# Fox attention: one of four modulation vectors summed on GpSimd instead of VectorE

## The chip, the core and the metric

The kernel runs on one core of a Trainium2 chip. A core has TensorE (matmuls; PE in the profile, with PEld for its weight loads), VectorE (DVE), ScalarE (ACT), GpSimd (POOL) and SyncE (SP), whose queue issues all of this kernel's DMAs in order. The metric is the device time of one execution in microseconds, lower is better.

## What is computed

A trunk of two layers over 1024 tokens of 1024 channels: layer 0 mixes tokens by forgetting attention (16 heads of 64), layer 1 by gated linear attention, each followed by a SwiGLU network. Every sub-layer is modulated by six vectors of 1024 numbers, computed from one conditioning vector `c`:

```python
c_act = jax.nn.silu(c)
for i in range(DEPTH):
    mod = c_act @ ada_w[i] + ada_b[i]              # ada_w[i]: 1024 x 6144
    sh1, sc1, g1, sh2, sc2, g2 = jnp.split(mod, 6, axis=-1)
    h = modulate(rms_norm(x, norm1_g[i]), sh1, sc1)
    ...
    x = x + g1[:, None, :] * y
    h = modulate(rms_norm(x, norm2_g[i]), sh2, sc2)
    x = x + g2[:, None, :] * swiglu(h, ffn_w_in[i], ffn_w_out[i])
```

In the attention, per head and block of 128 queries, the logits are the scaled scores plus differences of a cumulative sum, masked causally; then softmax, then the product with the values.

## The kernel before

Matmuls run in three passes over a high and a low part of each operand (`mm3`, L285; the parts are made by `split` and by the weight loads, L205). Layer 0's attention runs in eight pairs of heads, `attention(p)` (L1207). A pair has two heads `a` and for each four units `g` in the order 0, 3, 1, 2 (L1195); a unit is two query blocks, 2g and 2g+1. `scores(u)` (L1112) of a unit does, for each of its two blocks: score matmuls (L1132, L1133) and a mask matmul (L1135) on TensorE; the sum with the cumulative row and a running minimum on VectorE (L1138); the exponential on ScalarE (L1142); the reciprocal of its sum on VectorE (L1143); and the division, which multiplies the row of probabilities by that reciprocal on GpSimd (L1144), in place, 128 x 128 up to 128 x 1024 numbers. The unit before it is then finished (`finish`, L1199; `outputs`, L1147): transposes of the probabilities (L1164), their split on ScalarE and VectorE (L174, L175), products with the values (L1176, L1178), and the sum into the output tile (L1193). The probabilities live in a ring of three slots, `lpr`.

Beside pair p's attention, `weave` (L130) lays the projections for pair p+1: queries and keys (`qk_proj`, L1097), evacuated by `q_evac` and `k_evac` (L760, L770: two clearings on GpSimd, copies on ScalarE, differences on VectorE), and values (`v_half`). Beside pair 7 it lays the first part of the output projection (`fox_tail`, L1307). Attention with these runs from about 102 to 612 us of the span; then come the rest of the output projection and the two SwiGLU networks with the second mixer between them.

Weights are loaded as 512 KB tiles into a ring of three slots, `wr`, and split: the high part on ScalarE (L223), the low part in four quarters, three on GpSimd and one on VectorE (L227). Up to three weights are fetched ahead.

Two of layer 0's modulation vectors are made at the start. The other four, 2 to 5, are summed during the attention by `ada_steps` (L411). Each vector is the sum of 32 rows of 128 x 256 numbers; row o is a tile of `ada_w` times a column of the activated `c` (`c42`). One `ada_steps` loads four rows at a time by four DMAs of 128 KB (L423) into a slot of the same ring `wr`, and adds them on VectorE, one instruction a row (L442 the first, L444 the others). It ends with two small matmuls (L449) and an addition (L452). Vector 2 gates the attention's output (L1277, pair 7 and after), 3 and 4 modulate the second norm, 5 gates the SwiGLU network's output.

A `Pace` (L458) says where in the program these steps are called for: `ada0(3.3)` behind each of the projections of queries and keys from `qk_proj(2, 0)` on (L1108), twelve calls, each worth 3.3 steps; four vectors have 36 steps. The order of the instructions on each engine is made when the program is built: a scheduler takes from all that its model of the engines holds ready, the earlier in the program first, so an instruction can run well ahead of the place where it is called for, if its data and its slot are there. Data, ring slots and a few written orders (`in_order`, the lags of `weave` on TensorE) bound this. On the chip each engine's order is fixed.

Of the kernel before, what the change touches and what calls it, by code (L numbers as in the profile page):

```python
# [9 lines left out]
F32 = mybir.dt.float32  # L10
# [4 lines left out]
ALU = mybir.AluOpType  # L15

P = 128
S = 1024
D = 1024
ND = D // P  # L20
HALF = 512
# [32 lines left out]
def trunk(ctx, tc, x, c, ada_w, ada_b, norm1_g, norm2_g, ffn_w_in, ffn_w_out,  # L54
          fox_w_in, fox_b_f, fox_w_out, gla_w_in, gla_w_a2, gla_b_a, gla_g_o,
          gla_w_out, final_g, out, dbg=None, stop=None):
    nc = tc.nc
# [51 lines left out]
    def psl(t, n=1):  # L109
        return slice(t * P, (t + n) * P)  # L110
# [55 lines left out]
    four = cst.tile([P, 4], F32, name="four")  # L166
# [104 lines left out]
    class Weights:  # L271
# [36 lines left out]
    acc_r = Ring(big, acc_sl)  # L308
# [65 lines left out]
    for t in range(6):  # L374
        nt, src = (4, rows2[0:8, :]) if t < 4 else (2, crow)
# [4 lines left out]
    vec = cst.tile([P, 160], F32, name="vec")  # L380
    cact = cst.tile([P, 8], F32, name="cact")
    c42 = cst.tile([P, 64], F32, name="c42")
# [10 lines left out]
    modc = cst.tile([P, 2, 6, 8], F32, name="modc")  # L393
# [8 lines left out]
    def make_a(l, i, ks=slice(0, 8)):  # L402
        j = 1 if i == 0 else 4
        g0 = 96 + i * 16 + l * 8
        nc.vector.scalar_tensor_tensor(amul[:, l, i, ks], modc[:, l, j, ks], 1.0,
                                       vec[:, g0:g0 + 8][:, ks], op0=ALU.add, op1=ALU.mult)

    def last_of(e):
        return next(i for i in reversed(nc.cur_bb.bb.instructions) if i.engine == ENG[e])

    def ada_steps(l, j, acc, raw_of, nt, ahead):  # L411


        steps, got = deque(range(32 // nt)), deque()

        def load():
            if not steps:
                return
            n = steps.popleft()
            raw = raw_of([P, nt * 256], F32, f"ada{l}{j}{n}").rearrange("p (t c) -> p t c", t=nt)  # L420
            src = ada_w[l, 32 * nt * n:32 * nt * (n + 1), j * D:(j + 1) * D]
            for q in range(4):
                nc.sync.dma_start(raw[32 * q:32 * q + 32],  # L423
                                  src[:, 256 * q:256 * q + 256].rearrange("(r t) c -> r t c", t=nt))
            got.append(raw)

        for _ in range(ahead):
            load()
        for n in range(32 // nt):
            load()  # L430
            if ahead:
                yield ADA_A
            raw = got.popleft()
            with ExitStack() as es:
                if ahead:
                    es.enter_context(tc.issue_after(last_of("D")))
                elif n == 0:
                    es.enter_context(tc.issue_after(split_after["D"]))
                for t in range(nt):
                    o = (0 if nt == 4 else 32) + t * (32 // nt) + n  # L440
                    if n == t == 0:
                        nc.vector.tensor_scalar(acc, raw[:, t], c42[:, o:o + 1], None, op0=ALU.mult)  # L442
                    else:
                        nc.vector.scalar_tensor_tensor(acc, raw[:, t], c42[:, o:o + 1], acc,  # L444
                                                       op0=ALU.mult, op1=ALU.add)
            yield ADA_B if ahead else 1.0
        mp = pj([P, 2, 4], F32, f"mp{l}{j}")
        for b in range(2):
            nc.tensor.matmul(mp[:, b], acc[:, psl(b)], four, start=True, stop=True)  # L449
        o = l * 48 + j * 8  # L450
        qb = lambda t: t.rearrange("p (q b) -> p b q", b=2)
        nc.vector.tensor_add(qb(modc[:, l, j]), mp, qb(vec[:, o:o + 8]))  # L452
        for i, jj in ((0, 1), (1, 4)):
            if j == jj:
                make_a(l, i)
        yield 1.0

    class Pace:  # L458
# [18 lines left out]
            while self.q:  # L477
                self(1.0)

    ada0, ada1 = Pace(), Pace()  # L480

    def ada1_queue(js, acc, raws_):
        r = Cycle(raws_)
# [254 lines left out]
    sr, tr, orr, pj = ps_rings(2, 3, 1, 2)  # L738
# [8 lines left out]
    def qk_tiles(p):  # L747


        at = {nm: qk_free.popleft() for nm in ("QA", "QB", "KA")}  # L750
        if p:
            before = qk_at.pop(p - 1)
            at.update(zip(("KB", "KLA", "KLB"), (before[nm] for nm in ("QA", "KA", "KLA"))))
            qk_free.extend(before[nm] for nm in ("QB", "KB", "KLB"))
        else:
            at.update({nm: qk_free.popleft() for nm in ("KB", "KLA", "KLB")})
        qk_at[p] = at
        return {nm: big.tile([P, S], FR, tag=sl, name=f"{nm}{p}") for nm, sl in at.items()}
# [202 lines left out]
    def load_cum(h):  # L961
        cums[h] = cumr([P, S], F32, f"cum{h}")
        nc.sync.dma_start(cums[h], cum_d[h].partition_broadcast(P))
# [82 lines left out]
    for n, (d, hf) in enumerate(rest0):  # L1046
# [23 lines left out]
        if n in late_tr:  # L1070
            tp, i = late_tr[n]
# [25 lines left out]
    def qk_proj(p, i):  # L1097

        if i == 0:
            qkt[p] = qk_tiles(p)  # L1100
        wt = feed.next()
        feed.depth = 3
        for hf in range(2):
            ps = pj([P, HALF], F32, f"qk{i}{p}{hf}")
            yield from proj(ps, wt, hT, hf)
            (k_evac if i else q_evac)(ps, qkt[p], hf)
        if p > 1:
            ada0(3.3)  # L1108

    oTs = {}  # L1110

    def scores(u):  # L1112

        p, a, g = u
        t = qkt[p]
        Qs, K1, KL = (t["QA"], t["KA"], t["KLA"]) if a == 0 else (t["QB"], t["KB"], t["KLB"])
        cm = cums[2 * p + a]
        if g < 2:
            both = lpr([P, (4 * g + 3) * P], F32, f"lp{p}{a}{g}")
            lps = [both[:, 0:(2 * g + 1) * P], both[:, (2 * g + 1) * P:]]  # L1120
        else:
            lps = [lpr([P, (2 * g + 1 + i) * P], F32, f"lp{p}{a}{g}{i}") for i in range(2)]
        st = sm.tile([P, 2, 4], F32, tag="st", bufs=4, name=f"st{p}{a}{g}")
        for qi in range(2):
            qb = 2 * g + qi
            qs, lp, Wd, mcur = psl(qb), lps[qi], (qb + 1) * P, 3e38
            cuts = (0, 384, 640) if Wd == 640 else (0, Wd) if Wd <= HALF else (0, HALF, Wd)
            for n_, (k0, k1) in enumerate(zip(cuts, cuts[1:])):
                ps = sr([P, k1 - k0], F32, f"s{p}{a}{qb}{k0}")
                early = u == (0, 0, 0)  # L1130
                diag = k1 == Wd
                nc.tensor.matmul(ps, Qs[:, qs], K1[:, k0:k1], start=True, stop=False)  # L1132
                nc.tensor.matmul(ps, Qs[:, qs], KL[:, k0:k1], start=False, stop=not diag)  # L1133
                if diag:
                    nc.tensor.matmul(ps[:, k1 - k0 - P:], identb, maskb, start=False, stop=True)  # L1135
                mnew = st[:, qi, n_:n_ + 1]
                with tc.issue_after(v_last) if early else ExitStack():
                    nc.vector.tensor_tensor_reduce(lp[:, k0:k1], ps, cm[:, k0:k1], 1.0, mcur,  # L1138
                                                   ALU.add, ALU.min, mnew)
                mcur = mnew  # L1140
                yield max(0.22, 0.00085 * (k1 - k0))
            nc.scalar.activation(lp, lp, AF.Exp, bias=mcur, scale=-1.0, accum_out=st[:, qi, 2:3])  # L1142
            nc.vector.reciprocal(st[:, qi, 3:4], st[:, qi, 2:3])  # L1143
            nc.gpsimd.tensor_scalar(lp, lp, st[:, qi, 3:4], 1.0, op0=ALU.mult, op1=ALU.mult)  # L1144
        return lps
# [61 lines left out]
    def attention(p):  # L1207
        for a in range(2):
            for g in ORDER:
                u = (p, a, g)  # L1210
                lps = yield from scores(u)
                if pending[0] is not None:
                    yield from finish(*pending[0])
                pending[0] = (u, lps)
        if p == 7:
            yield from finish(*pending[0])
# [2 lines left out]
        for g in gs:  # L1219
            yield from g  # L1220

    acc0 = acc_r([P, 2, HALF], F32, "acc0")[:, 0, 0:256]
    for j in (2, 3, 4, 5):
        ada0.q.append(ada_steps(0, j, acc0, wr, 4, 0))
    run(v_half(0, 0, gates_end))
    q_evac(accs[1][1][1], qkt[0], 1)
# [4 lines left out]
    for p in range(7):  # L1231
# [4 lines left out]
        load_cum(2 * p + 2)  # L1236
        load_cum(2 * p + 3)
    ada0.flush()


    def dump(name, tiles):
# [555 lines left out]
    pj, atr, kvr, opr, trr = ps_rings(3, 1, 1, 2, 1)  # L1797
# [336 lines left out]
```

## Time and profile before

| what | us |
|---|---|
| median of 3 executions (lowest, highest) | 2398.98 (2395.54, 2399.1) |
| the profiled execution, its own time | 2397.77 |
| its span, first to last instruction | 2396.1 |
| VectorE busy in the span | 1776.6 |
| GpSimd busy in the span | 1008.5 |

The profile is one execution. A row of a group gives line, engine, operation, out<-in with shapes and the count, then the busy time and the mean ns of one, then the idle time of the engine just before and what ended it. A row of the waits says who waited for whom: the sum in us, the times, the longest. A row of the timeline gives start, duration, engine and instruction; `[1.43 <-DMA ...]` is idle time before it and what ended that. PE's ends are modelled, so what its rows show for certain is when it started, and when it stood idle. The granted clock of TensorE is 0.997 of full speed over this execution.

### The profile page before, as it was taken

How to read it: one execution, taken by the hardware profiler on the slowest of the kernel's cores; microseconds unless marked ns; L12 is line 12 of the kernel's file. 1: busy time of each engine (PE TensorE's matmuls, PEld its weight loads, DVE VectorE, ACT ScalarE, POOL GpSimd, SP SyncE). 2: the span in 40 equal slices, each digit the busy share in tenths (PEclk: the TensorE clock that was granted, in tenths of full speed). 3: DMA queues.
4: the chain of work that ended last, by engine and by line, in shares of the span. 5: the costliest groups of instructions: out<-in, count | busy, mean ns of one | idle time of the engine just before them, and what ended most of it. 6: DMA issues, size and time to landing. Idle time of an engine off the chain costs nothing.

```text
span 2396.1 us, 35784 instructions
## 1 busy us (share of the span) xinstructions
PE 2368.3 (99%) x12344; PEld 2016.8 (84%) x12344; DVE 1776.6 (74%) x3016; ACT 1127.8 (47%) x2164; POOL 1008.5 (42%) x911
## 2 busy tenths in 40 slices
PE   8999999999999999999999999999999999999998
PEld 7888888888888888888888888898888888888888
DVE  6577878886698788876798666655687877775787
ACT  6666555674443333345325645353343333345326
POOL 1333333333445666643264321222345666643262
PEclk9999999999999999999999999999999999999999
DMA  7422424342435544557655242334424544457664
GB/s 254 145 89 90 131 84 128 106 138 83 150 109 173 179 166 165 171 196 261 229 187 162 67 119 80 107 112 135 136 96 161 183 145 159 154 182 256 228 202 146
DMA packets 335773, 363.42 MB, mean 152 GB/s; under 512 B 24348, under 2 KB 277432, under 8 KB 335592
## 3 DMA queue, kind: packets, MB, share of 16 engines
q1 hardware_dynamic: 335592, 361.15, 45.9%
q8 instruction: 97, 1.59, 0.3%
q14 instruction: 84, 0.69, 0.1%
HBM read 268.19 MB, written 92.86 MB: 151 GB/s over the span
## 4 chain that ended last, share of the span: by engine, by line
PE 90%; DVE 5%; DMA 2%; ACT 1%; issue 1%; POOL 0%; SPq 0%; DVEq 0%; POOLq 0%; ACTq 0%
PE p_b L288 16%; PE p_b L286 16%; PE p_b L287 16%; PE t_b L1164 2%; PE o_b L1178 2%; PE qk_b L286 2%; PE qk_b L287 2%; PE qk_b L288 2%; PE vps_b L286 1%; PE vps_b L288 1%; PE vps_b L287 1%; PE s_b L1132 1%; PE s_b L1133 1%; PE gr_b L286 1%; PE gr_b L287 1%
## 5 line engine op out<-in xcount | busy, mean ns | idle before, releaser
L175 DVE TENSOR_TENSOR o_s<-xv_s,o_s 128x512 fp32r<-128x512 f32 (+1 forms) x376 | 324.1, 867 | 66.1 <-ACT o_s L174 65.6
L174 ACT CAST o_s<-xv_s 128x512 fp32r<-128x512 f32 (+1 forms) x376 | 216.2, 587 | 303.6 <-PE p_b L288 248.0
L287 PE MATMUL p_b<-B,o_s 128*128 128x512 f32 x608 | 237.8, 391 | 0.0
L288 PE MATMUL p_b<-B,o_s 128*128 128x512 f32 x608 | 237.5, 391 | 0.0
L286 PE MATMUL p_b<-B,o_s 128*128 128x512 f32 x608 | 236.3, 392 | 0.0
L1144 POOL TENSOR_SCALAR lp_s<-lp_s,st 128x128 f32<-128x128 f32 (+7 forms) x128 | 99.0, 778 | 291.1 <-DVE st L1143 280.7
L843 POOL TENSOR_TENSOR ex_s<-xv_s,xv_s 128x512 f32<-128x512 f32 (+1 forms) x64 | 85.5, 1335 | 292.8 <-DMA xv_s<-in_ffn_w_in_dram 120.7
L286 PE MATMUL p_b<-T,o_s 128*128 128x512 f32 x480 | 186.7, 389 | 0.0
L287 PE MATMUL p_b<-T,o_s 128*128 128x512 f32 x480 | 186.7, 389 | 0.0
L288 PE MATMUL p_b<-T,o_s 128*128 128x512 f32 x480 | 181.2, 389 | 0.0
L287 PEld LDWEIGHTS p_b<-B,o_s 128*128 128x128 f32 x608 | 115.0, 189 | 23.9
L286 PEld LDWEIGHTS p_b<-B,o_s 128*128 128x128 f32 x608 | 115.0, 189 | 23.8
L288 PEld LDWEIGHTS p_b<-B,o_s 128*128 128x128 f32 x608 | 114.7, 189 | 24.0
L1142 ACT ACTIVATE lp_s<-lp_s,st 128x128 f32<-128x128 f32 (+7 forms) x128 | 99.3, 777 | 65.2 <-DVE st L1138 62.1
L174 ACT CAST pt_s<-t_b 128x512 fp32r<-128x512 f32 (+1 forms) x160 | 79.7, 547 | 75.4 <-PE t_b L1164 73.9
L845 POOL TENSOR_TENSOR xv_s<-ex_s,xv_s 128x512 f32<-128x512 f32 (+1 forms) x64 | 88.1, 1377 | 60.7 <-DVE o_s L175 58.2
L1521 DVE TENSOR_TENSOR ex_s<-ex_s,p_b 128x512 f32<-128x512 f32 x140 | 93.7, 681 | 23.4 <-PE p_b L288 23.2
L227 POOL TENSOR_TENSOR w_l_s<-w__s,w_h_s 128x256 fp32r<-128x256 f32 x90 | 69.7, 803 | 94.7 <-ACT w_h_s L223 56.7
L175 DVE TENSOR_TENSOR pt_s<-t_b,pt_s 128x512 fp32r<-128x512 f32 (+1 forms) x160 | 96.2, 631 | 15.9 <-ACT pt_s L174 15.3
L287 PEld LDWEIGHTS p_b<-T,o_s 128*128 128x128 f32 x480 | 90.1, 188 | 18.7
L286 PEld LDWEIGHTS p_b<-T,o_s 128*128 128x128 f32 x480 | 90.1, 188 | 18.7
L288 PEld LDWEIGHTS p_b<-T,o_s 128*128 128x128 f32 x480 | 90.1, 188 | 18.6
(1954 smaller groups left out, 7392.9 us busy)
## 6 DMA issues: line engine op xcount, KB each, us to landing
xv_s<-in_ffn_w_in_dram SPq DMA_DIRECT2D x176, 256.0 KB, 3.3
hid_B<-x SPq DMA_DIRECT2D x70, 512.0 KB, 2.6
ad_s<-in_ada_w_dram SPq DMA_DIRECT2D x384, 64.0 KB, 2.4
hid_T<-x SPq DMA_DIRECT2D x36, 512.0 KB, 2.8
xv_s<-in_ffn_w_out_dram SPq DMA_DIRECT2D x96, 192.0 KB, 5.3
ada_s<-in_ada_w_dram SPq DMA_DIRECT2D x128, 128.0 KB, 2.8
xv_s<-in_ffn_w_out_dram SPq DMA_DIRECT2D x40, 256.0 KB, 2.9
T2o<-hid_T SPq DMA_DIRECT2D x18, 512.0 KB, 8.4
```

The costliest lines, as they stand in the source:

```text
L174: nc.scalar.copy(hi, src)
L175: nc.vector.tensor_sub(lo, src, hi.bitcast(F32))
L227: (nc.gpsimd if i < 3 else nc.vector).tensor_sub(lo[:, cs], rw[:, cs], hi[:, cs].bitcast(F32))
L286: nc.tensor.matmul(ps, ah, bh, start=start, stop=False)
L287: nc.tensor.matmul(ps, ah, bl, start=False, stop=False)
L288: nc.tensor.matmul(ps, al, bh, start=False, stop=stop)
L843: nc.gpsimd.tensor_add(s1, a21, a22)
L845: nc.gpsimd.tensor_sub(a11, s1, a11)
L1142: nc.scalar.activation(lp, lp, AF.Exp, bias=mcur, scale=-1.0, accum_out=st[:, qi, 2:3])
L1144: nc.gpsimd.tensor_scalar(lp, lp, st[:, qi, 3:4], 1.0, op0=ALU.mult, op1=ALU.mult)
L1164: nc.tensor.transpose(tp[:, i, :], lps[qi][:, psl(2 * b + jj)], ident)
L1521: nc.vector.tensor_add(d, d if src is None else dest(G, src), ps)
```

## The change

Vector 5 leaves VectorE. A new generator, `ada_pool`, sums it on GpSimd, in 16 rounds of two rows. Each row is a multiplication by its column, in place in the loaded tile (the first row: into the sum), and an addition to the sum. The rounds share one buffer, a half of the tile `acc0` that was free: four DMAs of 64 KB load it, and they are issued for the next round when the second row of a round is added. `ada0p(0.8)` calls for a step behind the scores of each unit from pair 1 on, so behind the two divisions of that unit: 34 steps at 0.8 a unit. `ada0` has three vectors left and is called with 2.4 in place of 3.3. The loading and the end of a vector become functions of their own.

```diff
+    def ada_load(raw, l, j, n, nt):
+        src = ada_w[l, 32 * nt * n:32 * nt * (n + 1), j * D:(j + 1) * D]
+        for q in range(4):
+            nc.sync.dma_start(raw[32 * q:32 * q + 32],
+                              src[:, 256 * q:256 * q + 256].rearrange("(r t) c -> r t c", t=nt))
+
+    def ada_end(l, j, acc):
...
+    def ada_pool(l, j, acc, raw):
+
+        raw = raw.rearrange("p (t c) -> p t c", t=2)
+        ada_load(raw, l, j, 0, 2)
+        yield 1.0
+        for n in range(16):
+            for t in range(2):
+                o = 32 + t * 16 + n
+                y = raw[:, t] if n or t else acc
+                nc.gpsimd.tensor_scalar(y, raw[:, t], c42[:, o:o + 1], 1.0, op0=ALU.mult, op1=ALU.mult)
+                if n or t:
+                    nc.gpsimd.tensor_add(acc, acc, y)
+                if t and n < 15:
+                    ada_load(raw, l, j, n + 1, 2)
+                yield 1.0
+        ada_end(l, j, acc)
+        yield 1.0
...
-    ada0, ada1 = Pace(), Pace()
+    ada0, ada0p, ada1 = Pace(), Pace(), Pace()
...
         if p > 1:
-            ada0(3.3)
+            ada0(2.4)
...
                 lps = yield from scores(u)
+                if p:
+                    ada0p(0.8)
                 if pending[0] is not None:
...
-    acc0 = acc_r([P, 2, HALF], F32, "acc0")[:, 0, 0:256]
-    for j in (2, 3, 4, 5):
+    acc0 = acc_r([P, 2, HALF], F32, "acc0")
+    ada0p.q.append(ada_pool(0, 5, acc0[:, 0, 256:512], acc0[:, 1]))
+    acc0 = acc0[:, 0, 0:256]
+    for j in (2, 3, 4):
         ada0.q.append(ada_steps(0, j, acc0, wr, 4, 0))
...
     ada0.flush()
+    ada0p.flush()
```

More of the change, by code (lines that the diff above doesn't have):

```diff
@@ L409, in last_of @@
         return next(i for i in reversed(nc.cur_bb.bb.instructions) if i.engine == ENG[e])
+    def ada_load(raw, l, j, n, nt):
[4 more added lines that the diff above has]
+    def ada_end(l, j, acc):
+        mp = pj([P, 2, 4], F32, f"mp{l}{j}")
+        for b in range(2):
+            nc.tensor.matmul(mp[:, b], acc[:, psl(b)], four, start=True, stop=True)
+        o = l * 48 + j * 8
+        qb = lambda t: t.rearrange("p (q b) -> p b q", b=2)
+        nc.vector.tensor_add(qb(modc[:, l, j]), mp, qb(vec[:, o:o + 8]))
+        for i, jj in ((0, 1), (1, 4)):
+            if j == jj:
+                make_a(l, i)
+    def ada_pool(l, j, acc, raw):
[14 more added lines that the diff above has]
+        yield 1.0
     def ada_steps(l, j, acc, raw_of, nt, ahead):
@@ L420, in load @@
             raw = raw_of([P, nt * 256], F32, f"ada{l}{j}{n}").rearrange("p (t c) -> p t c", t=nt)
[L421 to L424, printed above, removed]
+            ada_load(raw, l, j, n, nt)
             got.append(raw)
@@ L446, in ada_steps @@
             yield ADA_B if ahead else 1.0
[L447 to L455, printed above, removed]
+        ada_end(l, j, acc)
         yield 1.0
```

## The prediction, made before the result was known

> **What bounds the kernel now.** I read the page first, its busy shares and the shares of its chain, to see which engine sets the end.
>
> ```profile
> PE 2368.3 (99%) x12344; PEld 2016.8 (84%) x12344; DVE 1776.6 (74%) x3016; ACT 1127.8 (47%) x2164; POOL 1008.5 (42%) x911
> PE 90%; DVE 5%; DMA 2%; ACT 1%; issue 1%; POOL 0%; SPq 0%; DVEq 0%; POOLq 0%; ACTq 0%
> ```
>
> TensorE is busy for 2368.3 of 2396.1 us, so 27.8 us of idle time are all that any regrouping of other engines' work can give back in the whole kernel. Next I cut out the stretch in which the four modulation vectors are summed, and there read the table by windows and TensorE's waits.
>
> ```profile
> core 0: us, PE busy (x) PEld busy (x) DVE busy (x) ACT busy (x) POOL busy (x), PEclk, DMA share, GB/s
> 134.00:480.00 346.00, 340.65 (x2235) 300.49 (x2233) 274.87 (x706) 210.03 (x449) 128.37 (x174) 1.00 0.35 107
> ```
>
> ```profile
> PE s_b L1132 <- DVE st L1138: 1.8, 3, 1.2
> PE t_b L1164 <- POOL lp_s L1144: 1.7, 1, 1.7
> PE vps_b L286 <- DVE QB L767: 1.2, 1, 1.2
> PE qk_b L286 <- DVE KLB L780: 0.3, 1, 0.3
> ```
>
> In these 346 us TensorE idles 346.00 - 340.65 = 5.35 us, VectorE is busy 274.87/346 = 79% and GpSimd 37%. The columns of the waits are the sum, the count and the longest. VectorE ends 3.3 us of the idle time and one division on GpSimd 1.7 us. No weight is among the releasers: TensorE never waits here for a load or a split. One of these waits shows how a modulation row gets into the path (timeline, all engines, in order of time):
>
> ```profile
> 353.52 0.49 DVE L444 SCALAR_TENSOR_TENSOR acc_s<-ada_s,c,acc_s 128x256 f32<-128x256 f32 x1 [1.43 <-DMA ada_s<-in_ada_w_dram]
> ...
> 354.52 0.48 DVE L444 SCALAR_TENSOR_TENSOR acc_s<-ada_s,c,acc_s 128x256 f32<-128x256 f32 x1
> ...
> 354.91 0.16 DVE L1143 RECIPROCAL st<-st 128x1 f32<-128x1 f32 x1
> ...
> 355.24 0.95 POOL L1144 TENSOR_SCALAR lp_s<-lp_s,st 128x640 f32<-128x640 f32 x1 [9.01 <-DVE st L1143]
> ...
> 356.24 0.44 PE L1164 MATMUL t_b<-ident,lp_s 128*128 128x128 f32 x2 [1.70 <-POOL lp_s L1144]
> ```
>
> VectorE stood 1.43 us for a late load of a row; the reciprocal came behind it in its queue, the division behind the reciprocal, the transposes behind the division. That is the kind of stall which the change can remove from VectorE, and the kind which it can plant on GpSimd.
>
> **The change, part by part.**
>
> *Taken from VectorE: vector 5.* The costs come from the groups by line.
>
> ```profile
> L444 DVE SCALAR_TENSOR_TENSOR acc_s<-ada_s,c,acc_s 128x256 f32<-128x256 f32 x124 | 64.7, 522 | 18.6 <-DMA ada_s<-in_ada_w_dram 16.6
> L442 DVE TENSOR_SCALAR acc_s<-ada_s,c 128x256 f32<-128x256 f32 x4 | 2.4, 591 | 1.2 <-DMA ada_s<-in_ada_w_dram 1.2
> ```
>
> Four vectors are 124 + 4 = 128 rows, 64.7 + 2.4 = 67.1 us of VectorE. One vector is 31 x 0.522 + 0.591 = 16.8 us. TensorE sets the end, so what counts is its idle time: 5.35 us beside 67.1 us of row sums, or 0.08 us for each us of VectorE. That gives 16.8 x 0.08 = **-1.3 us**. The bounds are 0 (TensorE's waits have other causes) and -5.35 us (all of its idle time goes). I take -1.3, since three of the four vectors stay.
>
> *Added to GpSimd: 32 multiplies by a column and 31 additions, 128x256.* The nearest rows have the same shapes: the division's own 128x256 form and the additions that split weights.
>
> ```profile
> L1144 POOL TENSOR_SCALAR lp_s<-lp_s,st 128x256 f32<-128x256 f32 x10 | 4.9, 493 | 0.8 <-DVE st L1143 0.7
> L227 POOL TENSOR_TENSOR wv_0l_s<-wv_s,wv_0h_s 128x256 fp32r<-128x256 f32 x15 | 11.6, 795 | 0.4 <-ACT wv_0h_s L223 0.4
> ```
>
> A row is 0.49 + 0.80 = 1.29 us; the vector is 32 x 0.493 + 31 x 0.795 = 40.4 us, against 16.8 us saved on VectorE. GpSimd goes from 128.37 to some 168.8 of 346 us, 49%. Its room is seen in its waits:
>
> ```profile
> POOL lp_s L1144 <- DVE st L1143: 189.9, 56, 9.0
> ```
>
> It idles 189.9 us ahead of 56 divisions, 3.4 us each, more than two rows. So I cost the busy time at **0**. What hides it is this waiting; if the cover is gone (a row starts just as a reciprocal ends), one row of 1.29 us is laid ahead of a division, at the most 32 x 1.29 = 41 us. Whether TensorE sees that depends on the spare time between a division and its transposes:
>
> ```profile
> 303.86 1.02 POOL L1144 TENSOR_SCALAR lp_s<-lp_s,st 128x896 f32<-128x896 f32 x1 [2.00 <-DVE st L1143]
> ...
> 307.00 0.50 PE L1164 MATMUL t_b<-ident,lp_s 128*128 128x128 f32 x3
> ```
>
> Here the division ends at 304.88 and the transposes start at 307.00: 2.1 us spare. At the end of a pair (355.24 above: ends at 356.19, transposes at 356.24) it is 0.05 us.
>
> *The loads: 16 rounds of four, into one buffer.* Vector 5 now has 64 issues on SP where it had 32, of half the size, and round n+1 can't be issued until the last addition of round n.
>
> ```profile
> 264.14 2.48 SPq L423 DMA_DIRECT2D ada_s<-in_ada_w_dram  x4
> ```
>
> ```profile
> DMA to landing us min/median/max: 2.5/2.8/4.2
> ```
>
> ```profile
> DVE acc_s L444 <- DMA ada_s<-in_ada_w_dram: 16.6, 12, 2.7
> DVE acc_s L442 <- DMA ada_s<-in_ada_w_dram: 1.2, 1, 1.2
> ```
>
> Four issues take 2.48 us and the last lands some 2.8 us behind its issue: 5 us in which GpSimd has nothing of this vector to do, then 2 x 1.29 = 2.6 us of rows. A round is at least 7.6 us, sixteen some 120 us, which fits. The multiply that waits for a load is the new wait: behind it on GpSimd stand divisions, weight splits and the clearing of key tiles, and behind those the transposes. VectorE, with three buffers, found 13 of 32 loads late, 17.8 us in all, 1.37 each, 2.7 at worst. With one buffer I take all 16 as late, by 1.37 us: 22 us of standing, of which TensorE feels what goes over the spare time. A stand of 1.37 us by itself is inside 2.1 us; only where the spare is nearly nothing does it come through, and such places are the six pair ends among the 48 units of pairs 1 to 6. I take 3 of the 16 loads at 1.37 us: **+4.1 us**. Bounds: 0 (divisions lie ahead of the multiplies), and 16 x 2.7 = 43 us.
>
> *SP's queue.* 32 more issues at 2.48/4 = 0.62 are 20 us of issuing, and the queue now stands for GpSimd's additions, with weight, cumulative-sum and row loads behind. It stands already:
>
> ```profile
> SPq L423 <- DVE w_l_s L227: 54.0, 11, 8.9
> ```
>
> Stands up to 8.9 us long leave no weight among TensorE's releasers, so I cost this at 0; the eight weight-ring slots that vector 5 gives up speak for less waiting there. Without that cover it would be the next late thing, by about one round's 2.48 us of issues ahead of a weight.
>
> *The other pacing* (2.4 for 3.3, three vectors for four) spreads 27 steps over the twelve calls that took 36: 0. The two matmuls and the addition that finish vector 5 stay as they are.
>
> *A rule against the change.* The same timeline, without TensorE, shows a row sum under a division:
>
> ```profile
> 242.57 0.48 DVE L444 SCALAR_TENSOR_TENSOR acc_s<-ada_s,c,acc_s 128x256 f32<-128x256 f32 x1
> 242.71 2.06 POOL L1144 TENSOR_SCALAR lp_s<-lp_s,st 128x1024 f32<-128x1024 f32 x2 [0.95 <-DVE st L1143]
> ...
> 243.09 1.23 DVE L444 SCALAR_TENSOR_TENSOR acc_s<-ada_s,c,acc_s 128x256 f32<-128x256 f32 x1
> ```
>
> The row sum that began under the division took 1.23 us, the one before it 0.48. The Trainium skill, "SBUF — State Buffer", section "Who interferes with whom", says that a VectorE instruction with two SBUF inputs and a GpSimd one that reads SBUF lock each other out, the later for the whole of the earlier; by that rule the 1.23 us are explained, the trace agrees, and the rows added to GpSimd hold up the 96 row sums that stay. What it would do to the sum is the third rival.
>
> *Sum:* -1.3 + 0 + 4.1 + 0 = +2.8 us. The profiled execution took 2397.77 us, 1.7 over its span of 2396.1 and 1.2 under the median of 2398.98. Forecast: 2397.77 + 2.8 = **2400.6 us**; this case's own range is 2394 to 2406. About 0.2%, 4.8 us, is what a measurement of this kernel can tell from no change, so the forecast counts as none.
>
> **The rivals.**
>
> 1. *Slower: GpSimd's queue is parked on the single buffer.* If the order on GpSimd has a multiply right ahead of a division most times, a division comes late by the load's lateness and one row, 1.37 + 1.29 - 2.1 = 0.56 us over the spare time at the mean lateness, 2.7 + 1.29 - 2.1 = 1.9 at the worst: 9 to 30 us over 16 rounds. It decides from a lateness of 2.1 - 1.29 = 0.8 us on. For it: the 13 late loads on VectorE. Against it: the long idle time ahead of divisions, in which a stand is free. Some 15 us less the 1.3 gained: 2411.5 us. Chance 0.30.
>
> 2. *Faster: the stalls through VectorE were the rows' doing.* With a quarter fewer rows, reciprocals and evacuations come earlier and TensorE's 5.35 us close: 2392.4 us. For it: the stall at 354. Against it: that row belongs to a vector that stays. Chance 0.12.
>
> 3. *The lock-out gives VectorE's time back.* If every added GpSimd instruction holds up a two-input one of VectorE for its whole length, 40.4 us go against 16.8: VectorE loses 23.6 us net, at 0.08 us each +1.9 us in place of -1.3, so 2397.77 + 1.9 + 4.1 = 2403.8 us. Against it: only the row sums and some weight splits have two SBUF inputs. Chance 0.05.
>
> 4. *The change doesn't do what it says.* The rows are called for one by one behind the divisions of pairs 1 to 6, but nothing but their data ties them there. The trace has a precedent:
>
> ```profile
> 137.26 10.87 SPq L423 DMA_DIRECT2D ada_s<-in_ada_w_dram  x12
> ...
> 169.59 0.37 POOL L1144 TENSOR_SCALAR lp_s<-lp_s,st 128x128 f32<-128x128 f32 x1 [0.51 <-DVE st L1143]
> ```
>
> The first loads of vector 2, called for within pair 1, were issued at 137.26, ahead of that pair's first division at 169.59. So the rows may run in a bunch, as fast as the rounds of 7.6 us let them, from before 170 to about 290 us. The time is then that of the forecast or of rival 1; it has no chance of its own.
>
> **How the numbers follow.** Forecast 0.53 (0.01 faster, 0.47 within 0.2%, 0.05 slower), rival 1 0.30 (slower), rival 2 0.12 (0.10 faster, 0.02 within), rival 3 0.05 (0.02 within, 0.03 slower). Together: faster 0.11, same 0.51, slower 0.38. The range takes in rival 2's time and rival 1 up to a little over its middle: 2392 to 2414, leaving out about 0.15 above and some hundredths below.
>
> **What would show it.** VectorE's row sums fall from 128 to 96 and its busy time by 13 to 17 us in the stretch; GpSimd gains 63 instructions of 0.5 and 0.8 us, about 40 us. The step on loads shows as GpSimd idle ahead of the multiplies, ended by the row loads: 16 waits, about 22 us. TensorE's waits for divisions go from 1.7 to about 5 us; over 10 us is rival 1. Wrong would be a weight among TensorE's releasers (SP's queue), TensorE's idle time going below 2 us (rival 2), or a difference behind 620 us, where no step of mine acts.

## The result, and the profile after it

| | before | changed |
|---|---|---|
| median of 6 executions each, us (lowest, highest) | 2398.28 (2394.74, 2399.77) | 2413.84 (2408.19, 2417.89) |
| the profiled execution, its own time, us | 2397.77 | 2417.89 |
| its span, us | 2396.1 | 2415.7 |

The ratio is 1.0068, with a 95% interval of 1.0053 to 1.0084: slower by 15.6 us. The profiled execution of the changed kernel is the slowest of its six, so its trace has to explain some 20 us and not 15.6. Line numbers have moved: the division L1144 is now L1168, its reciprocal L1143 is L1167, the transposes L1164 are L1188, the row sums L442 and L444 are L474 and L476, the loads L423 are L414. New are the multiply L437 and the addition L439 on GpSimd.

First the page's busy shares and chain:

```profile
PE 2377.1 (98%) x12344; PEld 2023.9 (84%) x12344; DVE 1764.5 (73%) x2984; ACT 1128.9 (47%) x2164; POOL 1042.6 (43%) x974
PE 85%; DVE 4%; DMA 3%; POOL 2%; ACT 2%; SPq 2%; issue 2%; DVEq 0%; POOLq 0%; ACTq 0%
```

The work is as planned: 63 instructions more on GpSimd (974 for 911) and 34.1 us more of it, 32 fewer on VectorE and 12.1 us less. TensorE's share of the chain fell from 90% to 85%; GpSimd and SP's queue, at 0% before, came in with 2% each, and DMA rose from 2% to 3%. Where the new instructions ran, their two groups say (each row: instructions, shortest/median/longest ns, first and last start in us; then what ended the idle time before them):

```profile
L437 POOL TENSOR_SCALAR acc_s<-acc_s,c x32: 472/478/984, 74.0 to 203.2; 128x256 f32<-128x256 f32 x32
...
  DMA acc_s<-in_ada_w_dram: 37.3, 13
```

```profile
L439 POOL TENSOR_TENSOR acc_s<-acc_s x31: 722/733/900, 78.6 to 206.6; 128x256 f32<-128x256 f32 x31
```

The program calls for these rows behind the units of pairs 1 to 6. They ran in one bunch from 74 to 207 us: through the value projection ahead of the attention, all of pair 0 and the first head of pair 1. Thirteen of the sixteen rounds found GpSimd standing for their load, 37.3 us in all, 2.9 us each. The windows show where TensorE lost it (columns as in the prediction: window, us, then busy of PE, PEld, DVE, ACT, POOL, then PEclk, the granted clock, the DMA share and GB/s). After, the whole attention, the stretch shown of before, and four parts:

```profile
100.00:640.00 540.00, 522.45 (x3269) 454.84 (x3269) 382.02 (x971) 309.99 (x657) 221.41 (x315) 0.98 0.31 99
134.00:480.00 346.00, 335.88 (x2189) 296.14 (x2187) 254.77 (x653) 202.00 (x435) 144.70 (x210) 0.99 0.31 98
...
120.00:140.00 20.00, 16.06 (x117) 15.67 (x115) 8.49 (x29) 7.63 (x17) 13.12 (x22) 0.83 0.25 83
200.00:220.00 20.00, 16.75 (x98) 13.91 (x98) 10.70 (x28) 9.70 (x22) 11.02 (x18) 0.96 0.34 104
220.00:240.00 20.00, 17.61 (x83) 14.39 (x84) 12.72 (x32) 9.73 (x20) 5.80 (x7) 0.84 0.30 91
240.00:260.00 20.00, 19.56 (x123) 16.74 (x123) 15.80 (x43) 11.26 (x25) 4.64 (x7) 0.94 0.19 58
```

and before, the attention and the first of these parts:

```profile
100.00:640.00 540.00, 532.25 (x3354) 463.60 (x3353) 406.80 (x1023) 319.53 (x675) 202.09 (x269) 1.00 0.34 108
...
120.00:140.00 20.00, 20.00 (x154) 19.01 (x155) 12.68 (x36) 12.40 (x27) 8.91 (x14) 1.00 0.12 40
```

Two things are to be seen. TensorE idles 540 - 522.45 = 17.6 us in the attention, where it idled 7.8. And behind its idle times it runs slower: the granted clock is 0.83, 0.96, 0.84 and 0.94 in four stretches that had 1.00, which is 20 x (0.17 + 0.04 + 0.16 + 0.06) = 8.6 us. Together 9.8 + 8.6 = 18.4 us, a little counted twice because a stretch's clock is a mean over its idle time too. The shift of the same TensorE instructions between the two traces (start after minus start before, median by stretches of 20 us) says the same: 0.0 us at 100, +7.2 from 120 to 160, +9.1 at 180, +13.2 at 200, +20.6 at 220, then slowly back to +17.2 at 420 and within 0.5 us of that to 1300. At 1320 a step of 3.0 us is added, which is taken up below.

**The first loss** is for the most part one division in pair 0 (timeline of after, all engines):

```profile
120.07 0.16 DVE L1167 RECIPROCAL st<-st 128x1 f32<-128x1 f32 x1
...
121.35 0.93 POOL L437 TENSOR_SCALAR acc_s<-acc_s,c 128x256 f32<-128x256 f32 x2 [2.44 <-DMA acc_s<-in_ada_w_dram]
122.25 1.52 POOL L439 TENSOR_TENSOR acc_s<-acc_s 128x256 f32<-128x256 f32 x2
123.75 2.35 POOL L1168 TENSOR_SCALAR lp_s<-lp_s,st 128x1024 f32<-128x1024 f32 x3
...
124.92 2.18 PE L1188 MATMUL t_b<-ident,lp_s 128*128 128x128 f32 x9 [3.94 <-POOL lp_s L1168]
```

The reciprocal was there at 120.2 us. GpSimd stood 2.44 us for a load, until 121.35, then did that round's two rows, and began the division at 123.75, 3.5 us late; TensorE stood 3.94 us. In the trace of before the same division had no spare time either: TensorE's transposes waited 0.72 us for it (timeline of before):

```profile
119.99 1.20 PE L1164 MATMUL t_b<-ident,lp_s 128*128 128x128 f32 x9 [0.72 <-POOL lp_s L1144]
```

A smaller loss lies just ahead: GpSimd stood 4.40 us for a load until 113.35, the 128x896 division began at 114.95 behind that round's rows, and TensorE stood 1.58 us for it, until 116.19.

**The second loss** goes through three queues (timeline of after):

```profile
202.75 0.93 POOL L437 TENSOR_SCALAR acc_s<-acc_s,c 128x256 f32<-128x256 f32 x2 [2.08 <-DMA acc_s<-in_ada_w_dram]
...
207.30 2.13 POOL L227 TENSOR_TENSOR w_l_s<-w__s,w_h_s 128x256 fp32r<-128x256 f32 x3
...
209.46 2.50 SPq L414 DMA_DIRECT2D ada_s<-in_ada_w_dram  x4
...
215.31 2.04 DVE L476 SCALAR_TENSOR_TENSOR acc_s<-ada_s,c,acc_s 128x256 f32<-128x256 f32 x4 [6.76 <-DMA ada_s<-in_ada_w_dram]
217.27 0.68 DVE L1162 CUSTOM_DVE_ANT_0 lp_s<-s_b,cum_s 128x512 f32<-128x512 f32 x1
...
218.02 0.50 PE L1156 MATMUL s_b<-KB,QB 128*128 128x512 f32 x1 [2.50 <-DVE st L1162]
```

GpSimd stood 2.08 us for its row. With that round's rows and four clearings of key tiles ahead of it, its part of a weight's split ran from 207.30 to 209.43; VectorE's quarter of the same split had started at 203.30. The split gives back the ring slot into which SP was to load rows of vector 2; SP issued them at 209.46. VectorE, whose queue had those rows next, stood 6.76 us for them, and behind them stood the score sum that TensorE needed: 2.50 us, and 0.76 us more at 219.81. TensorE's waits of the whole run name both, and one place more:

```profile
PE t_b L1188 <- POOL lp_s L1168: 8.5, 5, 3.9
...
PE qk_b L286 <- DVE KLB L804: 3.1, 2, 2.4
PE s_b L1156 <- DVE st L1162: 2.8, 2, 2.5
```

The place more is the evacuation of keys (KLB): 2.39 us until 238.89, some 30 us after the last row. What makes it late was not followed.

### The profile page after: what moved, and what is told of

Read it like the earlier page. It is cut to its first block, busy times and chain, and to the rows that moved or that the text cites. A ratio compares the mean times of both kernels' runs of the same rounds, so it can differ in the third digit from the quotient of the medians.

```text
span 2415.7 us, 35863 instructions
## 1 busy us (share of the span) xinstructions
PE 2377.1 (98%) x12344; PEld 2023.9 (84%) x12344; DVE 1764.5 (73%) x2984; ACT 1128.9 (47%) x2164; POOL 1042.6 (43%) x974
## 4 chain that ended last, share of the span: by engine, by line
PE 85%; DVE 4%; DMA 3%; POOL 2%; ACT 2%; SPq 2%; issue 2%; DVEq 0%; POOLq 0%; ACTq 0%
PE p_b L288 16%; PE p_b L287 16%; PE p_b L286 16%; PE o_b L1202 2%; PE t_b L1188 2%; PE qk_b L286 1%; PE qk_b L287 1%; PE qk_b L288 1%; SPq L414 1%; PE gr_b L286 1%; PE gr_b L287 1%; PE gr_b L288 1%; PE vps_b L288 1%; PE vps_b L287 1%; PE vps_b L286 1%
## 5 line engine op out<-in xcount | busy, mean ns | idle before, releaser
L1168 POOL TENSOR_SCALAR lp_s<-lp_s,st 128x128 f32<-128x128 f32 (+7 forms) x128 | 98.1, 772 | 257.8 <-DVE st L1167 252.3
L175 DVE TENSOR_TENSOR pt_s<-t_b,pt_s 128x512 fp32r<-128x512 f32 (+1 forms) x160 | 96.1, 631 | 20.6 <-ACT pt_s L174 20.2
L286 PEld LDWEIGHTS p_b<-T,o_s 128*128 128x128 f32 x480 | 90.1, 188 | 18.7
L287 PEld LDWEIGHTS p_b<-T,o_s 128*128 128x128 f32 x480 | 90.1, 188 | 18.7
L879 POOL TENSOR_TENSOR xv_s<-xv_s,xv_s 128x512 f32<-128x512 f32 x40 | 54.2, 1355 | 117.2 <-issue 73.3
```

Source lines behind the costliest of these rows:

```text
L175: nc.vector.tensor_sub(lo, src, hi.bitcast(F32))
L286: nc.tensor.matmul(ps, ah, bh, start=start, stop=False)
L287: nc.tensor.matmul(ps, ah, bl, start=False, stop=False)
L879: nc.gpsimd.tensor_sub(r[A12], r[A12], r[A11])
```

## The experiments

The theory: the rows run ahead of their place, each round stands on GpSimd for a load that can only be issued when the round before is done, and what stands behind it (divisions, weight splits, and through their ring slots SP's loads and VectorE's rows) is late; TensorE pays, and pays again in clock. The rivals: GpSimd's added busy time itself; the work taken from VectorE and its new pacing; the loads' traffic; something peculiar to GpSimd. All runs were timed against the kernel before on the same chip.

| kernel | us, median | ratio to before (95% interval) |
|---|---|---|
| the change | 2413.84 | 1.0068 (1.0053 to 1.0084) |
| each row ordered behind a unit's divisions | 2398.72 | 1.0005 (0.9995 to 1.0015) |
| only the first row ordered | 2410.68 | 1.0056 (1.0042 to 1.007) |
| vector 5 left out | 2397.28 | 1.0002 (0.9993 to 1.0011) |
| no reload | 2398.81 | 1.0005 (0.9996 to 1.0014) |
| reload after every second round | 2406.73 | 1.0034 (1.0021 to 1.0047) |
| the same rounds on VectorE | 2413.55 | 1.0063 (1.0048 to 1.0078) |
| vectors 2 to 4 left out | 2408.9 | 1.0043 (1.0027 to 1.006) |
| vector 5 on GpSimd, by the weight ring | 2403.89 | 1.0027 (1.0016 to 1.0037) |
| the same, each row ordered | 2408.69 | 1.0043 (1.003 to 1.0055) |
| loads issued by GpSimd | 2403.43 | 1.0017 (1.0008 to 1.0026) |

### Each row ordered behind a unit's divisions

```diff
-                nc.gpsimd.tensor_scalar(y, raw[:, t], c42[:, o:o + 1], 1.0, op0=ALU.mult, op1=ALU.mult)
+                with tc.issue_after(last_of("G")):
+                    nc.gpsimd.tensor_scalar(y, raw[:, t], c42[:, o:o + 1], 1.0, op0=ALU.mult, op1=ALU.mult)
```

> Every multiply of vector 5 is ordered on GpSimd behind the division traced just before it, so that rows can't run ahead of pair 1 any more; all work and all loads stay. Theory A (the rows ran in a bunch from 74 to 207 us, and a multiply that stood for its load held divisions and weight splits up): the cost goes, 2395 to 2403 us. Theory B (40 us more of GpSimd and its lock-out with VectorE cost wherever they are): still 2409 to 2416. Theory C (the other pacing of vectors 2 to 4 and a new order of everything cost the time): still about 2413.

Measured: 2398.72 us, 1.0005, no measurable difference from before. The group of the multiplies:

```profile
L438 POOL TENSOR_SCALAR acc_s<-acc_s,c x32: 468/478/895, 183.1 to 481.9; 128x256 f32<-128x256 f32 x32
...
  DMA acc_s<-in_ada_w_dram: 10.3, 4
```

The same rows, loads and buffer, called for at the same places, cost nothing that can be measured when they are held to those places: they run from 183 to 482 us, and four of them stand 10.3 us where thirteen stood 37.3. TensorE waits 3.5 us for divisions in the whole attention, 2.0 at the longest. The place is the cause, not the work.

### Only the first row ordered

```diff
+                with tc.issue_after(last_of("G")) if n == t == 0 else ExitStack():
+                    nc.gpsimd.tensor_scalar(y, raw[:, t], c42[:, o:o + 1], 1.0, op0=ALU.mult, op1=ALU.mult)
```

> Only the first multiply is ordered, behind the first division of pair 1; the other 31 may run as early as their data lets them. Theory A: the 7 us lost at 114 to 125 us (pair 0) go, and about half to all of the other 10 us are lost in pairs 1 and 2 instead: 2402 to 2411. Theory B or C: about 2413.

Measured: 2410.68 us, 1.0056. One multiply still runs at 73.9 us; it must be the first round's second, which nothing orders. The others run from 182.5 to 314 us, near where the prediction had put the bunch, and cost nearly as much. The shift is +0.1 us until 180, +6.5 at 220, +8.9 at 300 and +9.9 at 1300; a step of 3.5 at 1320 follows. The last of these losses, in the timeline of this kernel:

```profile
298.36 0.93 POOL L438 TENSOR_SCALAR acc_s<-acc_s,c 128x256 f32<-128x256 f32 x2 [4.46 <-DMA acc_s<-in_ada_w_dram]
299.27 0.80 POOL L1169 TENSOR_SCALAR lp_s<-lp_s,st 128x640 f32<-128x640 f32 x1
...
300.12 0.57 PE L1189 MATMUL t_b<-ident,lp_s 128*128 128x128 f32 x3 [3.63 <-POOL lp_s L1169]
```

A stand of 4.46 us ahead of a division, and TensorE idle for 3.63 us. So it isn't pair 0 that makes the bunch dear: in both places where it has lain, some of its stands met work without spare time.

### Vector 5 left out

```diff
-        raw = raw.rearrange("p (t c) -> p t c", t=2)
-        ada_load(raw, l, j, 0, 2)
...
+        nc.gpsimd.memset(acc, 0.0)
```

> Vector 5 is left out: its sum is set to zero on GpSimd, no row and no load of it, and vectors 2 to 4 keep the new pacing of 2.4. Shows what freeing VectorE of 32 rows is worth by itself. Theories A and B: 2393 to 2398, a gain of 1 to 5 us on the kernel before. Theory C: still above 2405.

Measured: 2397.28 us, 1.0002. VectorE is busy for 264.85 us between 134 and 480 us in place of 274.87, TensorE for 341.52 in place of 340.65, and the whole is worth nothing that can be measured. The interval allows a gain of 0.07%, 1.7 us: that bounds what freeing VectorE could bring. The new pacing of 2.4 is in this run too, so it is the two together that make no difference.

### No reload

```diff
-                if t and n < 15:
-                    ada_load(raw, l, j, n + 1, 2)
```

> As the change, but only the first round is loaded; the 15 other rounds multiply and add what lies in the buffer, so part of the sum is wrong. 63 instructions stay on GpSimd, unordered, and no row waits for a load but the first. Theory A (the waiting for loads is the price): 2395 to 2403, and no GpSimd idle time ahead of a multiply but the first. Theory B: 2405 to 2414.

Measured: 2398.81 us, 1.0005. The rows run unordered in a bunch from 73.6 to 136.0 us, and stand for no load. One loss is still there, in the same place as the first one of the change:

```profile
117.89 0.16 DVE L1165 RECIPROCAL st<-st 128x1 f32<-128x1 f32 x1
...
119.08 1.53 POOL L439 TENSOR_TENSOR acc_s<-acc_s 128x256 f32<-128x256 f32 x2
...
121.04 1.68 POOL L1166 TENSOR_SCALAR lp_s<-lp_s,st 128x1024 f32<-128x1024 f32 x2
...
122.22 1.08 PE L1186 MATMUL t_b<-ident,lp_s 128*128 128x128 f32 x7 [3.47 <-POOL lp_s L1166]
```

Rows and splits alone, back to back, bring this division 3 us behind its reciprocal; the shift rises by 4.1 us at 120. It is worked off later (+0.5 us at 640). So busy time in a bunch is not quite free in pair 0, though the theory had put it at nothing; it makes one loss that the rest of the attention takes back, and no second one. Two things weaken this run as a proof: its bunch is over by 136 us, ahead of the place of the second loss, and 60 of the 64 loads are gone with their traffic and issues. That these cost nothing by themselves is shown by the first experiment, which keeps them.

### Reload after every second round

```diff
-                if t and n < 15:
+                if t and n < 15 and n % 2:
```

> As the change, but only every second round is loaded anew (8 loads of 16; the other rounds use what lies in the buffer, so the sum is wrong). Theory A by the number of waits: between the change and the version without reloads, 2402 to 2409. If a few single places make the loss and not the number of loads: either 2396 to 2401 or 2410 to 2415.

Measured: 2406.73 us, 1.0034; seven stands, 20.7 us. With 1, 8 and 16 loads the time is 2398.8, 2406.7 and 2413.8 us: about 1 us for each load in which the next round must wait. That is an average and not a price: in this trace most of the loss is one place, a division for which TensorE stands 4.6 us, where the shift goes from -0.3 to +5.0 us (at 120); it ends at +5.9, with a step of 1.6 at 1320. So a time in the middle doesn't rule out that a few places make the loss.

### The same rounds on VectorE

```diff
-                nc.gpsimd.tensor_scalar(y, raw[:, t], c42[:, o:o + 1], 1.0, op0=ALU.mult, op1=ALU.mult)
-                if n or t:
-                    nc.gpsimd.tensor_add(acc, acc, y)
+                if n == t == 0:
+                    nc.vector.tensor_scalar(acc, raw[:, t], c42[:, o:o + 1], None, op0=ALU.mult)
+                else:
+                    nc.vector.scalar_tensor_tensor(acc, raw[:, t], c42[:, o:o + 1], acc,
+                                                   op0=ALU.mult, op1=ALU.add)
```

> The new generator with its single buffer and 16 loads, unordered, but on VectorE, one instruction a row as before. Theory A (a queue that stands for single-buffered loads, on whichever engine): VectorE stands at the loads with score sums and reciprocals behind it, 2403 to 2425. Theory B' (GpSimd's longer rows are needed for the loss): 2395 to 2401.

Measured: 2413.55 us, 1.0063, as slow as the change, with two fifths of its busy time (31 x 0.485 + 0.54 = 15.6 us) and none of it on GpSimd. Its first loss, in the timeline:

```profile
111.17 0.48 DVE L439 SCALAR_TENSOR_TENSOR acc_s<-acc_s,c 128x256 f32<-128x256 f32 x1 [4.71 <-DMA acc_s<-in_ada_w_dram]
111.57 0.15 DVE L1168 RECIPROCAL st<-st 128x1 f32<-128x1 f32 x1
...
111.83 1.04 POOL L1169 TENSOR_SCALAR lp_s<-lp_s,st 128x128 f32<-128x128 f32 x2 [8.51 <-DVE st L1168]
...
112.47 0.48 PE L1189 MATMUL t_b<-ident,lp_s 128*128 128x128 f32 x1 [4.12 <-POOL lp_s L1169]
```

Here the reciprocal stands behind the row, and the division behind the reciprocal. So the loss doesn't need GpSimd; what the two kernels have in common is the single buffer and the missing order. VectorE stands 21.8 us in 11 places for these loads, GpSimd stood 37.3 in 13: the loss doesn't follow the sum of the stands either.

### Vectors 2 to 4 left out

```diff
-    for j in (2, 3, 4):
-        ada0.q.append(ada_steps(0, j, acc0, wr, 4, 0))
+    nc.vector.memset(acc0, 0.0)
+    for j in (2, 3, 4):
+        ada_end(0, j, acc0)
```

> As the change, but vectors 2, 3 and 4 are left out (their sums are set to zero): no row sums on VectorE, none of their loads on SP; vector 5 on GpSimd stays unordered, with its 16 loads. Theory A1 (the standing queue delays divisions, and through weight splits and the load ring also the rows of vector 2 on VectorE): the 7 us lost at 114 to 125 us stay, the 10 us lost at 206 to 243 us go: 2400 to 2407. Theory A2 (all of the loss is divisions and splits held up on GpSimd itself): still 2408 to 2414. If the loads of vector 2 are what makes those of vector 5 late: 2395 to 2400.

Measured: 2408.9 us, 1.0043. This run does not tell what it was meant to tell. It was to show the direct path alone, without VectorE's rows to be made late, but the edit calls for the small matmuls that end vectors 2 to 4 ahead of the value projection: they ran at 84 us, and the first scores came early too, at 80. TensorE's rows there:

```profile
80.00 0.49 PE L1156 MATMUL s_b<-KA,QA 128*128 128x128 f32 x2 [3.40 <-ACT KA L801]
...
84.29 2.72 PE L420 MATMUL mp_b<-four,acc_s 128*128 128x4 f32 x12 [1.85 <-DVE acc_s L1251]
```

The shift is +12.5 us by 80 us already, the work of the edit and not of vector 5. It rises to +18.7 at 220 and falls to +11.6 at 640. How the loss divides between the two paths is not had from it.

### Vector 5 on GpSimd, by the weight ring

The kernel before, with vector 5's multiplies and additions on GpSimd, loaded like the other vectors, four rows at a time into the ring, as the last of the four.

```diff
...
+                    elif j == 5 and nt == 4:
+                        nc.gpsimd.tensor_scalar(raw[:, t], raw[:, t], c42[:, o:o + 1], 1.0, op0=ALU.mult, op1=ALU.mult)
+                        nc.gpsimd.tensor_add(acc, acc, raw[:, t])
...
```

> The kernel before with only the engine of vector 5 changed: its rows are multiplied and added on GpSimd out of the ring of three 4 KB slots that the weights share, four rows a load, called for behind vector 4 at the old pacing. Theory A: no row can run far ahead of its place and its loads are issued early, so 2394 to 2402. Theory B: 2405 and more.

Measured: 2403.89 us, 1.0027, above what was expected. GpSimd's rows, from 383 to 487 us, stand for loads in four places, 7.8 us. The ten executions spread from 2400.1 to 2407.1 us and the profiled one is the slowest, so what its trace shows need not be in all of them. There is one loss of 5.5 us in the attention, at 400 us:

```profile
390.36 0.37 SPq L209 DMA_DIRECT2D w__s<-in_fox_w_in_dram  x1
...
392.44 2.49 SPq L423 DMA_DIRECT2D ada_s<-in_ada_w_dram  x4
...
397.29 2.05 DVE L447 SCALAR_TENSOR_TENSOR acc_s<-ada_s,c,acc_s 128x256 f32<-128x256 f32 x4 [6.20 <-DMA ada_s<-in_ada_w_dram]
399.26 0.68 DVE L1141 CUSTOM_DVE_ANT_0 lp_s<-s_b,cum_s 128x512 f32<-128x512 f32 x1
...
400.00 0.50 PE L1135 MATMUL s_b<-KB,QB 128*128 128x512 f32 x1 [1.86 <-DVE st L1141]
```

SP had stood 4.5 us for GpSimd's addition that gives back the slot for the load at 390.36 (it ended at 390.33), and the rows' load at 392.44 follows a split that GpSimd ended at 392.41. This is the path of the change's second loss again, without the single buffer: rows late on GpSimd, slots given back late, VectorE standing 6.20 us for its rows.

### The same, each row ordered

Each multiply of the run before is ordered behind the instruction last called for on GpSimd.

```diff
...
+                        with tc.issue_after(last_of("G")):
+                            nc.gpsimd.tensor_scalar(raw[:, t], raw[:, t], c42[:, o:o + 1], 1.0, op0=ALU.mult, op1=ALU.mult)
...
```

> The kernel of the run before with vector 5 on GpSimd through the weight ring (2403.9 us unordered, with one 5.5 us step at 396 to 416 us), now with each multiply ordered behind the instruction last called for on GpSimd. The theory (what costs is a row standing ahead of work that TensorE waits for, on its engine or through a ring slot given back late): the rows lie behind divisions, the bunch at 383 to 487 us is gone, 2395 to 2400 us. The rival (the ring slots that GpSimd gives back late cost this much wherever the rows lie): 2402 to 2406 us.

Measured: 2408.69 us, 1.0043: outside what either expected, and the theory's number is missed by some 9 us. The rows now lie from 437 to 525 us, still a bunch, since this generator is called for inside the projections, four rows a step, and not behind divisions. The shift goes from -0.7 at 440 to +9.0 us at 540. SP stands 9.0 us for a slot, and in the timeline VectorE's quarter of a split takes 2.86 us beside GpSimd's work:

```profile
468.76 2.14 POOL L227 TENSOR_TENSOR w_l_s<-w__s,w_h_s 128x256 fp32r<-128x256 f32 x3
469.05 2.86 DVE L227 TENSOR_TENSOR w_l_s<-w__s,w_h_s 128x256 fp32r<-128x256 f32 x1 [1.89 <-ACT w_h_s L223]
...
478.46 0.55 PE L286 MATMUL qk_b<-h0h,w_h_s 128*128 128x512 f32 x1 [2.27 <-DVE KLB L786]
```

How these two come to TensorE was not followed. An order as such, then, heals nothing. What the first experiment had beside the order was a place for each row, one behind a unit's divisions, and a buffer that no weight waits for. Which of the two was worth more isn't separated by these runs.

### Loads issued by GpSimd

```diff
-        ada_load(raw, l, j, 0, 2)
+        ada_load(raw, l, j, 0, 2, nc.gpsimd)
...
-                    ada_load(raw, l, j, n + 1, 2)
+                    ada_load(raw, l, j, n + 1, 2, nc.gpsimd)
```

> The changed kernel with vector 5's 64 loads issued by GpSimd in place of SP; the rows stay unordered and the buffer single. It takes away SP's queue standing for GpSimd's additions (22.6 us in 8 stands) and with it the late loads of vector 2 and of weights; GpSimd's own stand for its loads remains. The theory (both stands cost, the direct one at 115 to 130 us and the one through SP at 200 to 240 us): the first loss of 7 to 9 us stays, the later one goes, 2403 to 2410 us. The rival (all of the loss is the direct stand ahead of divisions and splits): 2411 us or more. If SP's queue is all of it: 2396 to 2401 us.

Measured: 2403.43 us, 1.0017 (1.0008 to 1.0026). The number is in the theory's range, but not for its reason: the first loss is the one that goes, and a later one stays. The rows stay unordered, from 74 to 242 us, but GpSimd stands only 6.7 us in 4 places for its loads, and TensorE's longest wait for a division is 1.9 us. The timeline of GpSimd shows why:

```profile
104.26 2.18 POOL L414 DMA_DIRECT2D acc_s<-in_ada_w_dram  x4
109.94 1.01 POOL L1168 TENSOR_SCALAR lp_s<-lp_s,st 128x896 f32<-128x896 f32 x1 [3.51 <-DVE st L1167]
110.94 0.92 POOL L437 TENSOR_SCALAR acc_s<-acc_s,c 128x256 f32<-128x256 f32 x2
```

Between a load and its rows there is now a division; in the change the rows stood there. The edit moved two things, SP's queue and the order on GpSimd, so it doesn't price SP's part. It suggests that the rows lose little where something else fills the load's flight: from 80 to 200 us the shift stays within 0.3 us, in spite of 34 us of issuing (64 of 0.53 us) that GpSimd does besides. At 220 us TensorE waits 2.4 us for an evacuation of keys on VectorE and the shift is +4.4; by 1300 us it is back at +0.9, and 3.2 us come at 1320.

## Why the prediction was wrong

Forecast was +2.8 us, no measurable change; it came out at +15.6. The time is nearly that of rival 1 (2411.5 us, chance 0.30), but by luck: rival 1 let a division come late in most of 16 rounds, and TensorE's waits for divisions are five in the whole run, 8.5 us (2.4 before), and 3.0 us in the prediction's own stretch, 134 to 480, where it had expected about 5 for the forecast and over 10 for rival 1. The rest came by the second path, the clock and the step at 1320. The place is nearly that of rival 4, and the range, to 2414, holds the median by a hair.

- **"The loads ... I take 3 of the 16 loads at 1.37 us: +4.1 us"** is the term that failed, in both factors. The lateness was 37.3/13 = 2.9 us, twice that of the nearest row, whose loads had three buffers where these have one; with one buffer VectorE's own rows stood 21.8/11 = 2.0 us. The runs don't divide the rest. And 1.37 us was laid against a spare time of 2.1 us read at one division; the first loss met a division whose spare was nothing, and it wasn't a pair end. That the stands for loads carry most of the loss the runs show: without reloads 2398.8, with half of them 2406.7, with all 2413.8 us; and only out of place, since with all loads and each row in its place it is 2398.7.
- **The count of places** looked at GpSimd's divisions in pairs 1 to 6 alone. About half of the loss, from +9.1 to +20.6 us at its height, came otherwise: GpSimd's late weight split, a ring slot, SP's load of vector 2, and 6.76 us of VectorE, with the clock and the wait for keys at 238.89 on top. Each link was within the prediction's reach: to ask what waits for the weight splits, one link further, would have found it.
- **Rival 4** was right that the rows would run in a bunch, and wrong to give that no time and no chance of its own, and to start it "before 170". Nothing but the first load held them, and they ran from 74 us: their buffer was their own, and its first load was issued at 66.8 us. The precedent was held by more: vector 2's first loads need slots of the weights' ring and were issued only at 137.26, and the first four rows of each vector have a written order in `ada_steps` (L438), which `ada_pool` leaves out. With the rows held to their places the forecast would have been right: 2398.7 us.
- **VectorE freed, -1.3 us:** no gain that can be measured; with the rows left out altogether the ratio is 1.0002. Its interval, -1.7 to +2.6 us, holds the -1.3 as well as the bound of 0, so the run doesn't decide between them.
- **GpSimd's busy time, 0:** its amount was nearly right (predicted 40.4; the medians give 32 x 0.478 + 31 x 0.733 = 38.0, the page's total rose by 34.1), and so was its price over the whole run, though its path there had a loss of 4 us in pair 0 that was worked off.
- **SP's queue, 0:** wrong in what it looked at. No weight became a direct releaser of TensorE, as predicted; but rows of vector 2 did come late behind SP's stands, and VectorE with them. **The other pacing, 0:** nothing in the runs speaks against it.
- **Not in any step: what an idle time costs behind itself.** The granted clock fell behind the long ones: some 8.6 us, beside 9.8 us of idle time, in the attention.
- **"A difference behind 620 us" would be wrong:** there is one, 3.0 us at 1320 us, at the second mixer's first projection. It is in six of the ten other kernels too, as 3.2 to 3.5 us, and in a seventh as 1.6; among the six is the one with each row ordered, which had gained 2.8 us until there and ends at no difference. One weight's load comes later there (ScalarE's wait for it, after and before):

```profile
1330.53 1.14 ACT L223 CAST w_h_s<-w__s 128x512 fp32r<-128x512 f32 x2 [4.57 <-DMA w__s<-in_gla_w_in_dram]
```

```profile
1312.28 1.15 ACT L223 CAST w_h_s<-w__s 128x512 fp32r<-128x512 f32 x2 [3.18 <-DMA w__s<-in_gla_w_in_dram]
```

SP issued the last weight load ahead of this copy at 1325.50 us after and at 1308.85 before, at the same place in its queue: 5.0 and 3.4 us ahead of the copy. Why it took longer is open, and no run here was made for it. So 3.0 of the profiled execution's 20 us are not explained.

## What to carry to other kernels

Where only data tie a piece of side work to its place, assume that it runs as early as its data allow, and price that case: either order it behind the instructions in whose shadow it is meant to lie, or give it other work between each load and its use. A single buffer on an engine's queue can turn each load's flight into a stand of everything behind it; follow that list through every slot the late instructions give back, not only to the nearest consumer. And ask first, by leaving the work out, what moving it could gain: here that was nothing measurable. An order alone is no cure, as the ring with ordered rows shows: the place must be one with time to spare.

## What the runs showed of the hardware

TensorE ran at about half speed behind an idle time of a few us. After the stall at 218 to 220 us, the 128x512 matmuls (timeline of the change, TensorE) start 427 ns apart (ten steps from 220.37 to 224.64), and from 225 on 230:

```profile
220.37 0.63 PE L287 MATMUL qk_b<-h0l,w_h_s 128*128 128x512 f32 x1
...
224.64 0.63 PE L288 MATMUL qk_b<-h0h,w_l_s 128*128 128x512 f32 x1
...
225.44 0.40 PE L287 MATMUL qk_b<-h0l,w_h_s 128*128 128x512 f32 x1
225.67 0.40 PE L288 MATMUL qk_b<-h0h,w_l_s 128*128 128x512 f32 x1
```

Twelve such matmuls cost 12 x 0.2 = 2.4 us, nearly as much as the 3.3 us of idle time before them. The Trainium skill, "TensorE: Matmul & The Clock Gate", Part 1, has the half rate, and puts its start at an idle window of about 3.4 us; the trace agrees on the rate, but had it after 2.50 and 0.76 us with three matmuls between, and behind an idle time of 2.39 us that ended at 238.9 (the row of 0.94 above). An idle time of 1.70 us in the kernel before and one of 2.03 us in the first experiment left the clock at 1.00; one of 1.84 us in the second, at 225 us, did not (0.83 from 220 to 230 us). A sharp bound isn't to be had from these.

A VectorE addition of a weight's split was long beside GpSimd's: 2.86 us in the row shown of the ring with ordered rows, where the shortest of its kind in that run took 0.41. Beside GpSimd's three quarters of the same split (2.13 us back to back) it took 2.27 us at 194.82 in the first experiment, and 2.27 at 320.18 in the kernel before. This fits the lock-out of the prediction's third rival, but it was there ahead of the change; above 2 us it comes twice in the kernel before, four times in the change and five times in the first experiment, which loses nothing measurable. So it doesn't explain the loss.
